# The SSD's new state in another accumulation bank, the first query block's attention on one bank

## The chip, the cores and the metric

The kernel runs on one core of one Trainium2 chip. The metric is device time in microseconds (us) of one execution, as a median of runs; a profile of one execution is there beside it.

## The reference, cut to what matters

One decoder layer over 2048 tokens of width 1024, in float32. Three groups of heads read one shared projection of the normalised input, and their outputs are joined, projected by `w_out` and added to the stream; two more blocks (SwiGLU and a gated embedding) follow.

```python
def _ssd(...):                                 # 6 heads x 64, state 128, chunks of 128
    scores = einsum("bclhn,bcshn->bclsh", cc, bc) * lmat
    y_diag = einsum("bclsh,bcshp->bclhp", scores, xc)
    states = einsum("bclhn,bclh,bclhp->bchpn", bc, decay_s, xc)
    # scan over chunks: carry * dec + st
    y_off = einsum("bclhn,bchpn,bclh->bclhp", cc, prev, exp(acs))
def _forgetting_attention(q, k, v, log_f):     # 6 heads x 64, causal
    logits = q k^T * scale + cum[q] - cum[k];  probs = softmax(masked logits);  out = probs v
...
h = h + concat([y_ssd, y_lru, y_fox]) @ w_out
h = h + (silu(u @ w_gate) * (u @ w_up)) @ w_down
```

## The kernel before, in words

The tokens are worked in four blocks `tb` of 512. Three phases follow each other. `phase1` makes the values, the queries and the RG-LRU for all blocks. `phase1b` runs over the blocks again: it projects `w_xbc`, convolves, runs the SSD in four chunks of 128 tokens (`ssd_chunk`), and makes `w_z` and the keys. `phase3` holds the SwiGLU and the gated embedding, with the attention of query blocks 1 to 3 threaded between its products.

Every large product is made in three passes of 512 columns (high by high, high by low, low by high, lines L201 to L203 in `mm3`, or L214, L215, L219 in `mm3_pair`). These products form the stream of TensorE, written to three accumulation banks with the tag `mm`. The other five banks have one tag each, `xa` to `xe`, and one buffer per tag: whoever writes the bank next waits until the last reader of its content is done.

Attention of query block 0 (`attention(0, ...)`) is a side job. It is started in `phase1b` at `tb == 1` and advanced one step at a time by `Side.tick` while products are recorded. For each of its six heads `scores` handles four query tiles: two products per tile (L642, L643) into the next bank of `tags`, read by VectorE into `lg` with the row's maximum (L647); then maximum, exponential on ScalarE (L654), reciprocal (L656) and scaling (L657). `outputs` takes four key tiles: transposes of `lg` into the next bank (L673), a rounded copy `ph` by ScalarE (L676), the remainder by VectorE (L677), and two products with the values into `xe` (L678, L679). A head ends with L682, L683 and a store to `dy` (L684). The tiles `kx`, `cum`, `lg` and `vc` of a head have one buffer.

`ssd_chunk` uses two banks. In `xa` stand, one after the other, the transposed input (L536, read by L552 and L554), the product with the old state (L563, read by L564) and the new state's product (L568, read by L574); in `xb` stand B by C (L539, L541), the diagonal part (L577) and the transposed result (L584).

At `tb == 3` (the last block) `load_y(0)` is recorded ahead of the SSD chunks. After five of eight tiles it runs `side.finish()`, which records all that is left of the side job, loads the three attention tiles from `dy`, and normalises them (square sums, `rms` in bank `xd`: L139, L141, L143, L145, L151, L153, then L832). The tiles feed `mix`, the product with `w_out`. For its first three output tiles the passes for the first five inputs can run ahead of the attention tiles; all else of the stream from there on stands behind them.

The text of the program doesn't fix the order of the instructions. A scheduler replays the recorded program against its own estimates and lays down one order per engine; each engine then works through its own list strictly in that order.

Of the kernel before, what the change touches and what calls it, by code (L numbers as in the profile page):

```python
# [12 lines left out]
F32R = mybir.dt.float32r  # L13
# [6 lines left out]
P = 128  # L20
# [3 lines left out]
TB = 512  # L24
# [40 lines left out]
class Trunk:  # L65
# [364 lines left out]
    def phase1b(self, ctx):  # L430

        nc, tc, a = self.nc, self.tc, self.a
        pool = lambda name, bufs, **kw: ctx.enter_context(tc.tile_pool(name=name, bufs=bufs, **kw))
        one = pool("m2one", 1)
        two = pool("m2two", 2)
        self.load_mpar(one)
        hcw = self.t(one, [P, 35], "hcw")
        nc.vector.tensor_scalar(hcw, self.pc("scw", 0, 35), 0.5, None, op0=ALU.mult)
        self.neg = self.t(one, [P, P], "neg")
        nc.sync.dma_start(self.neg, a["cst"][:, 2])  # L440
        self.tri = self.t(one, [P, P], "tri")
        nc.sync.dma_start(self.tri, a["cst"][:, 1])
        halo = self.t(one, [P, 7, 3], "halo")
        nc.gpsimd.memset(halo, 0.0)
        state = None
        for tb in range(NTB):
            if tb == 1:
                self.att_setup()
                self.side.start(self.attention(0, one, ("xc", "xd"), "xe"))
            u = []  # L450
            for k in range(KD):
                u.append(self.parts(k, self.load(self.du[tb, k]), nc.gpsimd))
            small = self.decays(tb, two)
            xbc = []
            for b in range(7):
                if b == 0:
                    pair = self.mm3_pair([self.weight(a["w_xbc"][i], KD) for i in range(2)], u)
                ps = pair[b] if b < 2 else self.mm3(self.weight(a["w_xbc"][b], KD), u, 3)
                xbc.append(self.conv(ps, halo[:, b], hcw[:, 4 * b:4 * b + 4], hcw[:, 28 + b:29 + b],
                                     two, (two, f"xbc{b}", 1) if tb % 2 and b else (self.hp, "h", None), True))  # L460
            ys = [self.t(two, [P, TB], f"ys{j}", bufs=1) for j in range(3)]
            if tb == NTB - 1:

                yx = self.load_y(0)
            for c in range(NCH):
                state = self.ssd_chunk(c, xbc, small, state, ys, two)
            if tb == NTB - 1:
                h = [self.mix(0, c, yx) for c in range(KD)]
                self.first = h, self.norm_split(h, "g2", eng=nc.vector, tag="xd")
            for b in range(3):  # L470
                ps = self.mm3(self.weight(a["w_z"][b], KD), u, 3)
                z = self.t(two, [P, TB], "t0")
                nc.scalar.activation(z, ps, ACT.Tanh, scale=0.5)
                nc.vector.scalar_tensor_tensor(z, z, 1.0, ps, op0=ALU.add, op1=ALU.mult)
                nc.vector.scalar_tensor_tensor(ys[b], ys[b], 0.5, z, op0=ALU.mult, op1=ALU.mult)
            for b in range(3):
                self.qk("w_k", b, tb, u, two)
            self.norm_store(ys, 384, 0, tb, "xa")
# [46 lines left out]
    def ssd_chunk(self, c, xbc, small, state, ys, two):  # L525
        nc = self.nc
        cs = slice(c * P, (c + 1) * P)
        xs, bm, cm = xbc[0:3], xbc[3:5], xbc[5:7]
        first = state is None
        dtc, ab, ex = small  # L530
        dt, ab = dtc[:, 0, c], ab[:, c]
        whole, dec, since = ex[:, 0, c], ex[:, 1, c], ex[:, 2, c]

        ptr = self.ps("xa", (P, 3, P))
        for j in range(3):
            nc.tensor.transpose(ptr[:, j], xs[j][:, cs], self.ident)  # L536
        pgb = self.ps("xb", (P, 4, P))
        for g in range(2):
            nc.tensor.matmul(pgb[:, g], lhsT=bm[g][:, cs], rhs=cm[g][:, cs], start=True, stop=True)  # L539
        for g in range(2):  # L540
            nc.tensor.transpose(pgb[:, 2 + g], bm[g][:, cs], self.ident)  # L541
        bt = self.t(two, [P, 2, P], "bt", bufs=1)
        nc.scalar.activation(bt, pgb[:, 2:4], ACT.Copy)

        cb = self.t(two, [P, 2, P], "cb", bufs=1)
        nc.vector.tensor_tensor(cb, pgb[:, 0:2], self.tri.unsqueeze(1).to_broadcast([P, 2, P]), op=ALU.mult)
        seg = self.t(two, [P, 6, P], "seg", bufs=1)
        nc.scalar.activation(seg, ab, ACT.Exp, scale=-1.0)

        px = ptr.rearrange("p j (i e) -> p (j i) e", i=2)  # L550
        xc = self.t(two, [P, 6, 64], "xc", bufs=1)
        nc.vector.tensor_tensor(xc, px, dt.unsqueeze(2).to_broadcast([P, 6, 64]), op=ALU.mult)  # L552
        xd = self.t(two, [P, 6, 64], "xd", bufs=1)
        nc.vector.tensor_tensor(xd, px, dec.unsqueeze(2).to_broadcast([P, 6, 64]), op=ALU.mult)  # L554
        for g in range(2):
            nc.gpsimd.tensor_tensor(seg[:, 3 * g:3 * g + 3], seg[:, 3 * g:3 * g + 3],
                                    cb[:, g].unsqueeze(1).to_broadcast([P, 3, P]), op=ALU.mult)

        yt = self.t(two, [P, 6, 64], "yt", bufs=1)
        if not first:  # L560
            pso = self.ps("xa", (P, 6, 64))
            for g in range(2):
                nc.tensor.matmul(pso[:, 3 * g:3 * g + 3], lhsT=cm[g][:, cs], rhs=state[:, 3 * g:3 * g + 3], start=True, stop=True)  # L563
            nc.vector.tensor_tensor(yt, pso, since.unsqueeze(2).to_broadcast([P, 6, 64]), op=ALU.mult)  # L564

        pst = self.ps("xa", (P, 6, 64))
        for g in range(2):
            nc.tensor.matmul(pst[:, 3 * g:3 * g + 3], lhsT=bt[:, g], rhs=xd[:, 3 * g:3 * g + 3], start=True, stop=True)  # L568
        ns = self.t(two, [P, 6, 64], "state")
        if first:  # L570
            nc.vector.tensor_copy(ns, pst)
        else:
            nc.gpsimd.tensor_tensor(ns, state, whole.unsqueeze(2).to_broadcast([P, 6, 64]), op=ALU.mult)
            nc.vector.tensor_tensor(ns, ns, pst, op=ALU.add)  # L574
        psd = self.ps("xb", (P, 6, 64))
        for h in range(6):
            nc.tensor.matmul(psd[:, h], lhsT=seg[:, h], rhs=xc[:, h], start=True, stop=True)  # L577
        if first:
            nc.vector.tensor_copy(yt, psd)
        else:  # L580
            nc.vector.tensor_tensor(yt, yt, psd, op=ALU.add)
        py = self.ps("xb", (P, 3, P))
        for j in range(3):
            nc.tensor.transpose(py[:, j], yt[:, 2 * j:2 * j + 2].rearrange("p a b -> p (a b)"), self.ident)  # L584
        for j in range(3):
            nc.vector.scalar_tensor_tensor(ys[j][:, cs], xs[j][:, cs], self.pc("dsk", j), py[:, j], op0=ALU.mult, op1=ALU.add)
        return ns
# [20 lines left out]
    def attention(self, qc, pool, tags, tag_o):  # L608
# [52 lines left out]
        def outputs(h):  # L661
# [7 lines left out]
            for kt in range(nkt):  # L669
                d = max(0, kt - qc * NCH)  # L670
                pt = self.ps(next(banks))
                for qi in range(d, NCH):
                    nc.tensor.transpose(pt[:, qi * P:(qi + 1) * P], probs[qi][:, kt * P:(kt + 1) * P], self.ident)  # L673
                sl = slice(d * P, TB)
                ph = self.t(pool, [P, 2, TB], "ph", F32R, bufs=min(3, len(tags)))
                nc.scalar.activation(ph[:, 0, sl], pt[:, sl], ACT.Copy)  # L676
                nc.vector.tensor_tensor(ph[:, 1, sl], pt[:, sl], ph[:, 0, sl].bitcast(F32), op=ALU.subtract)  # L677
                nc.tensor.matmul(po[:, sl], lhsT=vc[:, kt], rhs=ph[:, 0, sl], start=kt == 0, stop=False)  # L678
                nc.tensor.matmul(po[:, sl], lhsT=vc[:, kt], rhs=ph[:, 1, sl], start=False, stop=kt == nkt - 1)  # L679
                yield  # L680
# [7 lines left out]
        for h in range(6):  # L688
            yield from outputs(h)
            if h < 5:  # L690
                yield from scores(h + 1)
# [345 lines left out]
```

## Time and profile before

| what | value |
|---|---|
| median of 3 runs | 2848.45 us (2848.25 to 2850.45) |
| profiled execution, time | 2852.96 us |
| its span, first to last instruction | 2851.1 us |
| TensorE busy | 2745.6 us, 96% of the span |
| mean granted TensorE clock | 0.981 |
| `phase1b` in the trace | from about 300 to about 780 us |
| attention of block 0 | first product at 385.0 us, last at 648.3 us |
| VectorE, ScalarE, GpSimd busy | 53%, 46%, 53% |

The span is 1.9 us shorter than the profiled execution's own time, and that time is 4.5 us above the median. "PEclk" in a row of stretches is the clock that TensorE was granted, as a share of the full one. A row of a timeline gives start, duration, engine, line, operation, tiles, and in brackets the idle time of the engine before it and what ended it.

### The profile page before, as it was taken

To read this page: it belongs to the slowest core of one execution; us is meant where nothing else is said; L and a number is where in the kernel's file an instruction comes from. 1 tells how busy PE (TensorE), PEld (TensorE's weight loads), DVE (VectorE), ACT (ScalarE), POOL (GpSimd) and SP (SyncE) were. 2 spreads that over 40 slices of the span, in tenths; PEclk is the share of its full clock that TensorE was granted. 3 is DMA by queue.
4 is the path that set the end of the run, shared out by engine and by line. 5 is a ranking of instruction groups with operands and counts; after the bars stand their busy time and mean duration, and the time that the engine had idled before them with its cause. 6 is when DMAs were issued, how large, how long until landed. Compare 5 with 4: busy or idle time off the path is not lost.

```text
span 2851.1 us, 36994 instructions
## 1 busy us (share of the span) xinstructions
PE 2745.6 (96%) x12845; PEld 2285.6 (80%) x12845; DVE 1506.5 (53%) x2740; ACT 1299.5 (46%) x1977; POOL 1518.6 (53%) x1409
## 2 busy tenths in 40 slices
PE   7999999998999999999999999999899999999997
PEld 5877787787877888888788888878788888888886
DVE  6776446676544442547655435566564565412236
ACT  5555535544344543434555434446564443322234
POOL 6435677555544555554555645445356554544554
PEclk8999999998999999999999999999999999999999
DMA  5554544352367663434988734279896532322232
GB/s 186 184 182 143 181 165 152 119 157 95 126 199 212 199 191 122 138 126 145 260 238 256 216 112 151 102 218 276 260 268 203 164 133 103 126 97 97 96 98 72
DMA packets 319509, 467.97 MB, mean 164 GB/s; under 512 B 54196, under 2 KB 212948, under 8 KB 317780
## 3 DMA queue, kind: packets, MB, share of 16 engines
q1 hardware_dynamic: 319322, 465.60, 52.5%
q8 instruction: 102, 1.67, 0.2%
q14 instruction: 85, 0.70, 0.1%
HBM read 371.62 MB, written 93.88 MB: 163 GB/s over the span
## 4 chain that ended last, share of the span: by engine, by line
PE 71%; DMA 9%; DVE 6%; POOL 4%; ACT 4%; issue 3%; SPq 2%; DVEq 0%; POOLq 0%; ACTq 0%
PE mm L201 20%; PE mm L202 20%; PE mm L203 20%; POOL w L192 2%; DMA dp<-lg 1%; PE xd L793 1%; PE xd L792 1%; ACT ab L522 1%; PE mm L219 1%; DMA ab<-drow 1%; DMA kx<-dk 1%; PE mm L214 1%; PE mm L215 1%; ACT w L189 1%; POOL u L228 1%
## 5 line engine op out<-in xcount | busy, mean ns | idle before, releaser
L192 POOL TENSOR_TENSOR w<-wst,w 128x512 fp32r<-128x512 f32 x848 | 1148.5, 1377 | 896.1 <-ACT w L189 815.0
L201 PE MATMUL mm<-u,w 128*128 128x512 f32 (+1 forms) x3080 | 1207.2, 392 | 6.9 <-DVE h L489 3.6
L202 PE MATMUL mm<-u,w 128*128 128x512 f32 (+1 forms) x3080 | 1206.1, 392 | 0.6 <-DVE u L879 0.6
L203 PE MATMUL mm<-u,w 128*128 128x512 f32 (+1 forms) x3080 | 1204.9, 392 | 0.8 <-POOL w L192 0.8
L201 PEld LDWEIGHTS mm<-u,w 128*128 128x128 f32 x3080 | 582.5, 189 | 119.2 <-ACT u L227 2.2
L203 PEld LDWEIGHTS mm<-u,w 128*128 128x128 f32 x3080 | 582.2, 189 | 117.0 <-POOL w L192 1.9
L189 ACT ACTIVATE w<-wst 128x1024 fp32r<-128x1024 f32 (+1 forms) x424 | 440.2, 1039 | 512.6 <-PE mm L203 329.7
L202 PEld LDWEIGHTS mm<-u,w 128*128 128x128 f32 x3080 | 582.5, 189 | 109.8 <-DVE u L879 1.0
L788 ACT ACTIVATE ph<-pT 128x512 fp32r<-128x512 f32 (+2 forms) x234 | 119.1, 539 | 146.6 <-PE xd L793 68.7
L789 POOL TENSOR_TENSOR ph<-pT,ph 128x512 fp32r<-128x512 f32 (+2 forms) x108 | 119.7, 1115 | 106.3 <-ACT ph L788 82.8
L789 DVE TENSOR_TENSOR ph<-pT,ph 128x512 fp32r<-128x512 f32 (+2 forms) x126 | 110.2, 888 | 109.5 <-ACT ph L788 99.9
L165 DVE TENSOR_TENSOR ssq<-ssq,sq 128x512 f32<-128x512 f32 x125 | 123.9, 991 | 77.1 <-ACT sq L161 73.9
L879 DVE SCALAR_TENSOR_TENSOR u<-th,u 128x512 fp32r<-128x512 f32 x88 | 111.9, 1271 | 66.8 <-ACT u L878 66.8
L747 ACT ACTIVATE lg<-lg,m 128x1024 f32<-128x1024 f32 (+5 forms) x72 | 102.0, 1416 | 90.1 <-DVE m L745 89.0
L876 DVE TENSOR_TENSOR th<-th,mm 128x512 f32<-128x512 f32 x88 | 60.0, 682 | 155.7 <-PE mm L203 154.9
L751 DVE STREAM_TRANSPOSE lg<-lg 128x1024 f32<-128x1024 f32 (+5 forms) x72 | 113.4, 1576 | 42.9 <-ACT lg L750 42.7
L875 DVE SCALAR_TENSOR_TENSOR th<-th,mm 128x512 f32<-128x512 f32 x88 | 60.1, 682 | 130.7 <-ACT th L874 130.7
L874 ACT ACTIVATE th<-mm 128x512 f32<-128x512 f32 x88 | 52.3, 594 | 162.2 <-PE mm L203 161.0
L892 DVE TENSOR_TENSOR h<-h,mm 128x512 f32<-128x512 f32 x96 | 65.2, 681 | 102.8 <-PE mm L203 102.6
L792 PE MATMUL xd<-ph,vc 128*128 128x256 f32 (+1 forms) x396 | 106.8, 282 | 9.9 <-ACT ph L788 7.0
L793 PE MATMUL xd<-ph,vc 128*128 128x256 f32 (+1 forms) x396 | 103.4, 286 | 3.4 <-DVE ph L789 3.2
L750 ACT ACTIVATE lg<-lg,r 128x1024 f32<-128x1024 f32 (+5 forms) x72 | 101.7, 1412 | 10.7 <-DVE r L749 10.7
(319 smaller groups left out, 3313.7 us busy)
## 6 DMA issues: line engine op xcount, KB each, us to landing
wst<-in_w_gate SPq DMA_DIRECT2D x88, 512.0 KB, 3.7
wst<-in_w_up SPq DMA_DIRECT2D x88, 512.0 KB, 3.6
pT<-dp SPq DMA_DIRECT2D x162, 256.0 KB, 4.5
wst<-in_w_down SPq DMA_DIRECT2D x64, 448.0 KB, 3.5
wst<-in_w_out SPq DMA_DIRECT2D x32, 512.0 KB, 3.5
wst<-in_w_down SPq DMA_DIRECT2D x32, 512.0 KB, 5.4
wst<-in_w_pg SPq DMA_DIRECT2D x32, 512.0 KB, 3.5
vc<-dv SPq DMA_DIRECT2D x60, 256.0 KB, 4.8
```

Source lines behind the costliest of these rows:

```text
L165: (eng or nc.gpsimd).tensor_tensor(acc, acc, s, op=ALU.add)
L189: nc.scalar.activation(w[:, 0], st, ACT.Copy)
L192: nc.gpsimd.tensor_tensor(w[:, 1, k], st[:, k], w[:, 0, k].bitcast(F32), op=ALU.subtract)
L201: nc.tensor.matmul(ps, lhsT=w[:, 0, k], rhs=x[:, 0], start=k == 0, stop=False)
L202: nc.tensor.matmul(ps, lhsT=w[:, 0, k], rhs=x[:, 1], start=False, stop=False)
L203: nc.tensor.matmul(ps, lhsT=w[:, 1, k], rhs=x[:, 0], start=False, stop=k == len(u) - 1)
L751: nc.vector.transpose(lg, lg)
L788: nc.scalar.activation(hi, src, ACT.Copy)
L789: (nc.vector if t0 % 4 == 0 else nc.gpsimd).tensor_tensor(lo, src, hi.bitcast(F32), op=ALU.subtract)
L792: nc.tensor.matmul(po[:, sl], lhsT=vc[:, t0 + i], rhs=ph[:, 0, i, sl], start=t0 + i == 0, stop=False)
L793: nc.tensor.matmul(po[:, sl], lhsT=vc[:, t0 + i], rhs=ph[:, 1, i, sl], start=False, stop=t0 + i == KH - 1)
L879: nc.vector.scalar_tensor_tensor(hh[:, 1], th, 0.5, hh[:, 0].bitcast(F32), op0=ALU.mult, op1=ALU.subtract)
```

## The change

The product for the SSD's new state (L568) goes to bank `xd`, where it went to `xa`. The attention of query block 0, which used `xc` and `xd` in turn, uses `xc` alone. `ph` has two buffers, as it had (the smaller of 3 and the number of banks, which was 2). No arithmetic changes.

```diff
-                self.side.start(self.attention(0, one, ("xc", "xd"), "xe"))
+                self.side.start(self.attention(0, one, ("xc",), "xe"))
...
-        pst = self.ps("xa", (P, 6, 64))
+        pst = self.ps("xd", (P, 6, 64))
...
-                ph = self.t(pool, [P, 2, TB], "ph", F32R, bufs=min(3, len(tags)))
+                ph = self.t(pool, [P, 2, TB], "ph", F32R, bufs=2)
```

The scheduler lays down another order from the first of these instructions on. Three places follow; in the names, the first number is the tile's, and `h` and `xbc` are conv outputs, `lg0` to `lg3` the probabilities of the four query tiles.

TensorE, the outputs of the third head (its sum is `xe_911`), before: the transposes for two key tiles go to `xc` and `xd` in turn, in one piece at the end of a product of `mm_1201`.

```order
L568 MATMUL xa_858_4348<-xd_855_4339,bt_851_4331 128x192 x2
L577 MATMUL xb_860_4354<-xc_854_4337,seg_853_4335 128x64 x6
L673 MATMUL xc_912_4560<-ident_11_92,lg0_879_4452 128x128
L673 MATMUL xc_912_4560<-ident_11_92,lg1_886_4476 128x128
L673 MATMUL xd_914_4576<-ident_11_92,lg1_886_4476 128x128
L673 MATMUL xc_912_4560<-ident_11_92,lg2_893_4498 128x128
L673 MATMUL xd_914_4576<-ident_11_92,lg2_893_4498 128x128
L584 MATMUL xb_861_4362<-ident_11_92,yt_856_4343 128x128 x3
L673 MATMUL xc_912_4560<-ident_11_92,lg3_904_4534 128x128
L673 MATMUL xd_914_4576<-ident_11_92,lg3_904_4534 128x128
L678 MATMUL xe_911_4559<-ph_913_4565,vc_910_4557 128x512
L679 MATMUL xe_911_4559<-ph_913_4565,vc_910_4557 128x512
```

The same head's outputs now; the second key tile's transposes stand behind the first one's L679, and the SSD's L568 has its own bank.

```order
L536 MATMUL xa_1153_5541<-ident_11_92,h_1011_4985 128x128
L678 MATMUL xe_911_4559<-ph_913_4565,vc_910_4557 128x512
L568 MATMUL xd_1149_5520<-xd_1146_5511,bt_1142_5503 128x192 x2
L679 MATMUL xe_911_4559<-ph_913_4565,vc_910_4557 128x512
L673 MATMUL xc_914_4576<-ident_11_92,lg1_886_4476 128x128
L673 MATMUL xc_914_4576<-ident_11_92,lg2_893_4498 128x128
L673 MATMUL xc_914_4576<-ident_11_92,lg3_904_4534 128x128
L536 MATMUL xa_1153_5541<-ident_11_92,h_1015_5002 128x128
```

It moved from behind the 1704th product pass of `phase1b`'s and `phase1`'s stream to behind the 1844th.

TensorE, the end of the stream that can run ahead of the attention tiles (`mm_1401`, third tile of `mix`), before. All of attention lies ahead of these rows; behind them follow the norm of block 2's SSD output (`xa_1227`), one SSD chunk, and the attention tiles' norm (`xd_1325`, `xd_1330`).

```order
L203 MATMUL mm_1401_6699<-u4_1318_6384,w_1400_6695 128x512
L139 MATMUL xa_1227_5917<-ones_14_97,ssq_1224_5909 128x1 x4
...
L563 MATMUL xa_1344_6455<-state_1176_5617,xbc5_1295_6294 128x192
L563 MATMUL xa_1344_6455<-state_1176_5617,xbc6_1302_6342 128x192
L139 MATMUL xd_1325_6401<-ones_14_97,ssq_1322_6393 128x1 x4
L568 MATMUL xa_1345_6459<-xd_1342_6450,bt_1338_6442 128x192 x2
L584 MATMUL xb_1348_6473<-ident_11_92,yt_1343_6454 128x128 x3
```

The same place now: the rest of the fourth head (`xe_966`) and all of the fifth (`xe_1074`) and sixth (`xe_1193`) stand between `mm_1401`'s last early pass and the attention tiles' norm, with no product of the stream among them.

```order
L203 MATMUL mm_1401_6699<-u4_1318_6384,w_1400_6695 128x512
L678 MATMUL xe_966_4779<-ph_1023_5038,vc_965_4777 128x256
...
L642 MATMUL xc_1041_5117<-kx_1034_5102,qx_1036_5104 128x128
...
L679 MATMUL xe_1074_5235<-ph_1089_5313,vc_1073_5233 128x128
L642 MATMUL xc_1105_5376<-kx_1098_5361,qx_1100_5363 128x128
...
L679 MATMUL xe_1193_5685<-ph_1205_5750,vc_1192_5683 128x128
L139 MATMUL xd_1325_6401<-ones_14_97,ssq_1322_6393 128x1 x4
L153 MATMUL xd_1330_6414<-sq_1331_6415,ones_14_97 128x512
L153 MATMUL xd_1330_6414<-sq_1332_6418,ones_14_97 128x512
L201 MATMUL mm_1391_6629<-u5_1333_6422,w_1390_6625 128x512
```

The sixth head ended 68 passes ahead of `mm_1401`'s early end, and now ends behind it.

SyncE's queue, the last attention stores and the load of the last attention tile, now; before, the two stores lay with four loads of weights and one of `ab` between them.

```order
L665 DMA vc_1192_5683<-dv_3_83 128x4x128
L684 DMA dy_4_84<-ot_1090_5324 64x512
L684 DMA dy_4_84<-ot_1206_5761 64x512
L817 DMA ld_1321_6391<-dy_4_84 128x512
L817 DMA ld_1388_6621<-in_xt 128x512
```

The load of the last tile stands directly behind the last store; what moved is where in time the queue comes to them.

## The prediction

> **What bounds the kernel.** I read the page first, then the stretches around the change, then TensorE's timeline in them. The page says who carries the end: TensorE is busy for 96% of the span and holds 71% of the chain that ended last, so whatever adds to its idle or slow time is added to the end, and nothing else is.
>
> ```profile
> PE 2745.6 (96%) x12845; PEld 2285.6 (80%) x12845; DVE 1506.5 (53%) x2740; ACT 1299.5 (46%) x1977; POOL 1518.6 (53%) x1409
> PE 71%; DMA 9%; DVE 6%; POOL 4%; ACT 4%; issue 3%; SPq 2%; DVEq 0%; POOLq 0%; ACTq 0%
> ```
>
> The stretches of the second phase (start:end, length, busy time of the engines, granted clock, DMA share, GB/s) show where TensorE isn't saturated there.
>
> ```profile
> core 0: us, PE busy (x) PEld busy (x) DVE busy (x) ACT busy (x) POOL busy (x), PEclk, DMA share, GB/s
> 430.00:550.00 120.00, 117.12 (x589) 98.33 (x587) 76.17 (x180) 61.07 (x133) 83.16 (x120) 0.99 0.45 142
> 550.00:580.00 30.00, 23.71 (x103) 18.25 (x103) 25.36 (x63) 17.05 (x34) 15.33 (x14) 0.83 0.46 133
> 580.00:650.00 70.00, 68.34 (x363) 58.44 (x362) 46.53 (x122) 33.23 (x74) 37.15 (x61) 0.98 0.51 159
> 650.00:670.60 20.60, 18.00 (x81) 14.94 (x81) 15.46 (x27) 14.52 (x32) 12.63 (x19) 0.92 0.24 71
> 670.60:692.50 21.90, 15.47 (x67) 12.10 (x66) 14.25 (x30) 4.29 (x8) 6.18 (x5) 0.69 0.10 37
> ```
>
> The last row is the hole that matters. At 670.6 us the passes that need no attention tile are used up, and until 692.5 us TensorE has only the norm of the SSD output and one SSD chunk. Its two ends on TensorE, with the chain that closes it:
>
> ```profile
> 670.41 0.39 PE L203 MATMUL mm<-u,w 128*128 128x512 f32 x1
> 675.56 0.79 PE L153 MATMUL xa<-sq,ones 128*128 128x512 f32 x1 [0.85 <-DVE sq L151]
> 679.97 2.79 PE L577 MATMUL xb<-xc,seg 128*128 128x64 f32 x12 [0.74 <-DVE xc L552]
> 683.94 1.71 PE L139 MATMUL xd<-ones,ssq 128*128 128x1 f32 x8
> 692.49 0.97 PE L201 MATMUL mm<-u,w 128*128 128x512 f32 x3 [0.37 <-ACT u L171]
> ```
>
> So the hole lasts 692.49 - 670.64 = 21.9 us (670.64 is where the next instruction took over). Attention had ended well before it, and none of its work is in it.
>
> **The change, part by part.**
>
> The arithmetic, the instructions and their sizes stay. The buffer count of `ph` was 2 and is 2: nothing.
>
> *The SSD's own bank.* L568 no longer waits for L564, and the next chunk's L536 no longer for L574. The order shows the chunks 20 to 80 passes earlier in block 1, and up to 26 in block 2. They are side work beside a saturated stream, so this earns only what TensorE loses around them (below).
>
> *One bank for attention.* Each step must now go product, read, next product, where two banks let the next product run beside the read. In the order the third head's outputs fall back by 140 passes, and the rest of the fourth head with all of the fifth and sixth lands in the hole, with no pass of the stream to hide it. What is late next is the whole stream: `mix` needs the attention tiles. I price the new hole from row durations. By form (busy, mean ns), the steps of a head are:
>
> ```profile
> L647 DVE CUSTOM_DVE_ANT_0 lg<-xc,cd 128x128 f32<-128x128 f32 x12 | 3.4, 284 | 6.7 <-PE xe L679 6.5 <-POOL cd L634 0.2
> L647 DVE CUSTOM_DVE_ANT_0 lg<-xc,cum 128x256 f32<-128x256 f32 x6 | 2.5, 414 | 0.8 <-PE xc L643 0.7
> L647 DVE CUSTOM_DVE_ANT_0 lg<-xd,cum 128x384 f32<-128x384 f32 x6 | 3.3, 548 | 0.2 <-PE xd L643 0.2
> L654 ACT ACTIVATE lg<-lg,m 128x512 f32<-128x512 f32 x6 | 4.3, 722 | 7.0 <-DVE m L652 7.0
> L657 DVE TENSOR_SCALAR lg<-lg,r 128x512 f32<-128x512 f32 x6 | 5.2, 870 | 0.1
> L676 ACT ACTIVATE ph<-xc 128x512 fp32r<-128x512 f32 x6 | 3.6, 595 | 12.3 <-PE xc L673 12.3
> L676 ACT ACTIVATE ph<-xd 128x128 fp32r<-128x128 f32 x6 | 1.6, 274 | 0.7 <-PE xd L673 0.6
> L677 DVE TENSOR_TENSOR ph<-xc,ph 128x512 fp32r<-128x512 f32 x6 | 4.1, 687 | 2.9 <-ACT ph L676 2.9
> L677 DVE TENSOR_TENSOR ph<-xd,ph 128x128 fp32r<-128x128 f32 x6 | 1.7, 279 | 0.0
> L682 ACT ACTIVATE ot<-xe 64x512 f32<-64x512 f32 x6 | 3.6, 595 | 5.9 <-PE xe L679 5.8
> L683 DVE TENSOR_TENSOR ot<-xe,ot 64x512 f32<-64x512 f32 x6 | 4.1, 678 | 2.5 <-ACT ot L682 2.5
> ```
>
> TensorE's steps depend on its clock. In the timeline passes of 512 columns start 0.43 us apart after an idle stretch and 0.23 us apart when it is full; a lone pass of 512 lasts 0.79, so its result is out 0.36 us after its columns are through (0.17 by 0.40 at full clock).
>
> ```profile
> 554.67 0.79 PE L678 MATMUL xe<-ph,vc 128*128 128x512 f32 x1 [0.47 <-ACT ph L676]
> 561.45 0.63 PE L201 MATMUL mm<-u,w 128*128 128x512 f32 x1
> 561.88 0.63 PE L202 MATMUL mm<-u,w 128*128 128x512 f32 x1
> 565.41 0.40 PE L203 MATMUL mm<-u,w 128*128 128x512 f32 x1
> 565.64 0.39 PE L201 MATMUL mm<-u,w 128*128 128x512 f32 x1
> ```
>
> Scores of one head at half clock: products 2 x (0.11 + 0.21 + 0.32 + 0.43) + 4 x 0.36 = 3.6; reads, with the diagonal tile's 0.284 each time, 0.28 + 0.57 + 0.70 + 0.83, and 0.08 four times for the maximum = 2.7; the last tile's exponential 0.72 (with 0.4 for maximum, sum and reciprocal) and scaling 0.87 = 2.0. Outputs: transposes 1.1 + 4 x 0.36 = 2.5; the copies 0.60 to 0.27, summed along the sizes 1.7; the remainders 0.69 to 0.28, summed 1.9; the second products behind them 1.1 + 0.36 = 1.4. Some 20 hand-overs at 0.05 (the rows above start that much after their releaser ends) add 1.0. One head: 3.6 + 2.7 + 2.0 + 2.5 + 1.7 + 1.9 + 1.4 + 1.0 = 16.8 us. At full clock 4.5 less for the columns and results: 12.3.
>
> The hole then reads:
> - Until the fifth head's first product: the fourth head's end runs beside the norm, whose second L153 ends 676.35 - 670.64 = 5.7 after the stream; with the last remainder, 6.2.
> - The fifth head, 16.8, and the SSD chunk that its steps are interleaved with: L577 2.8 and three or four more small products of about 1 each, partly beside VectorE: 6.
> - The sixth head: 16.8.
> - The end: L682 0.6, L683 0.7, store 2.4, load 3.3, square and sum 1.4, and from L139 to the first pass 692.49 - 683.94 = 8.6: 17.0. The DMA rows (issue of the store and of the load that waits for it; the load's median to landing; and the issue of `cum`, ns, with its landing):
>
> ```profile
> 655.46 0.47 SPq L684 DMA_DIRECT2D dy<-ot  x1
> 657.81 0.33 SPq L817 DMA_DIRECT2D ld<-dy  x1
> ld<-dy SPq DMA_DIRECT2D x32, 256.0 KB, 3.3
> L628 SPq DMA_DIRECT2D cum<-dcum x6: 332/520/529, 385.4 to 605.4; - x6
> DMA to landing us min/median/max: 3.9/4.1/5.7
> ```
>
> That is 6.2 + 16.8 + 6 + 16.8 + 17.0 = 62.8 us at half clock, and 6.2 + 12.3 + 4 + 12.3 + 17.0 = 51.8 at full clock. The hole of before ran at 0.69 with a fuller TensorE, so I take 61, near the half-clock end. Upwards: the sixth head's keys load only once the fifth's scores are done, seven issues of about 0.5 us and some 4 us of landing against the 7.6 us of outputs that cover them; if these loads or slow forms of L657 come on top, 68. The term is 61 - 21.9 = **+39** (30 to 46).
>
> The Trainium skill ("TensorE: Matmul & The Clock Gate", Part 1) says that TensorE falls to half its clock after one idle window of about 3.4 us and needs as long a busy one to return. By that rule nearly all of this hole runs at half clock and the term is 41, by a gate that never closes it is 30. The 0.69 of the old hole agrees with a mixture that leans to the closed gate.
>
> *Work that leaves the covered part.* What the hole now does, the stream ahead of it no longer does. A head has 26 attention products; in the stream four of the smaller scores take 0.51 us together (592.91 to 593.42 below), so about 0.13 each, and the larger ones up to 0.23.
>
> ```profile
> 592.91 0.27 PE L642 MATMUL xc<-kx,qx 128*128 128x128 f32 x1
> 593.42 0.33 PE L577 MATMUL xb<-xc,seg 128*128 128x64 f32 x2
> ```
>
> 26 x 0.146 = 3.8 us per head, for 2.35 heads: **-8.9** (6.8 by columns alone to 11). One L568 and one L563 pair leave the hole for the later stream: **+0.8**.
>
> *Stalls ahead of the hole.* From 430 to 670.6 us TensorE idles 2.9 + 6.3 + 1.7 + 2.6 = 13.5 us, and the missing share of the clock, times the busy time, is 1.2 + 4.0 + 1.4 + 1.4 = 8. Half of that, 10.3, is in the one bunch of 550 to 580, which is exactly where the order shows the two-bank outputs piled up (TensorE waited there for `lg`, `ph` and `yt`). That bunch is dissolved. New bunches with one bank cost something back, because L679 now stands ahead of the next transposes in the list. **-8** (0 to -16).
>
> *GpSimd's list.* The next head's mask (L634) waits for `cum`, and the split of a weight of `mix` (L192) stands behind it. Fewer heads are done by then, so the waits fall among the passes that end the stream: **+2** (0 to 4).
>
> Sum: 39 - 8.9 + 0.8 - 8 + 2 = **+25 us**. The profiled execution would go from 2852.96 to 2878; against the median of the runs, 2848.45, I expect 2873.5. The ends together: 30 - 11 + 0.8 - 16 = +4, and 46 - 6.8 + 0.8 + 0 + 4 = +44; both ends need every term at its bound, so the range is 2856 to 2892.
>
> **The rivals.**
>
> A. *Keys and GpSimd stack up*: a wait takes the removed one's place at each head, for `cum` and `kx`. For it: in this trace each head loads its keys into the only buffer. Against it: seven issues fit in the outputs of one head. It gives 2892 to 2905.
>
> B. *The gate stays open and the stalls vanish*: the hole at full clock (+30) and all of the saving (-16) with -8.9 and +0.8 give +6, about 2854: the edge of no change.
>
> C. *Not slower: the unblocked SSD chunks empty the stalls ahead of the hole.* Place: 430 to 670 us. Price: at most the 21.5 us that the rows show, plus the 8.9 moved. It decides when the stalls saved exceed 39 - 8.9 + 0.8 = 31, and the rows hold only 21.5; only with the hole at its lower bound (30 - 8.9 + 0.8 = 22) do they meet. So about 2843 to 2850, and unlikely.
>
> D. *The second bank was never used*, since products are released by the ticks and not by banks. Then nothing ends later, and the time is within 0.2%. Against it stands the order, in which attention already ends late. The Trainium skill (the same page, "HAM oscillation") tells of a kernel in which double-buffering the accumulation banks gave no further gain (126.6 us to 125.5); the same here would mean about 2848.
>
> **How the numbers follow.** A measurement of this kernel can tell about 0.2% (5.7 us) from no change. Forecast, +8 to +44: 0.82. A: 0.07. B: 0.05, of which 0.02 lies within 0.2%. C: 0.04, of which 0.03 faster by more than 0.2%. D: 0.02, no change. Slower 0.92, same 0.05, faster 0.03. The range of 2856 to 2892 leaves out A, C, D and most of B.
>
> **What would show it.** Right: in the new profile a stretch of some 60 us, from about 650 to 715, in which TensorE is busy a third to a half with a clock of 0.5 to 0.7, chained L673, L676, L677, L679 and ended by L171; the stretch 550 to 580 fuller than before; all later stretches as before. Wrong: a hole under 50 us, attention's last L679 ahead of the last early pass of `mix`, or idle time in the third phase that isn't there now.

## The result, and the profile after

The changed kernel takes 2874.54 us (median of four runs, 2874.2 to 2875.35) against 2848.74 us: a ratio of 1.0089, 95% interval 1.0076 to 1.0102, so 25.8 us slower. The forecast was 2873.5. The profiled execution took 2874.38 us with a span of 2872.5.

The engines' totals hardly move; TensorE has the same 12845 products in 9 us more busy time, and its share of the chain falls from 71% to 68%.

```profile
PE 2754.8 (96%) x12845; PEld 2291.1 (80%) x12845; DVE 1498.5 (52%) x2740; ACT 1300.4 (45%) x1977; POOL 1519.2 (53%) x1409
PE 68%; DMA 10%; DVE 7%; ACT 5%; POOL 4%; issue 3%; SPq 2%; DVEq 0%; ACTq 0%; POOLq 0%
```

The stretches of the second phase, after (columns as in the prediction), with the new gap in the last row:

```profile
320.00:430.00 110.00, 104.07 (x487) 86.20 (x486) 48.72 (x97) 51.44 (x106) 78.95 (x116) 0.95 0.48 153
...
430.00:550.00 120.00, 115.86 (x565) 96.01 (x564) 78.55 (x165) 61.39 (x130) 87.89 (x121) 0.97 0.43 142
550.00:580.00 30.00, 30.00 (x151) 25.30 (x150) 17.04 (x39) 14.72 (x27) 15.44 (x16) 1.00 0.38 127
580.00:650.00 70.00, 67.36 (x348) 57.29 (x346) 49.17 (x115) 36.59 (x82) 45.79 (x75) 0.95 0.49 153
650.00:659.00 9.00, 9.00 (x50) 7.79 (x49) 6.10 (x14) 5.50 (x11) 2.21 (x3) 1.00 0.01 2
659.00:717.30 58.30, 32.85 (x102) 21.49 (x100) 26.14 (x88) 13.86 (x34) 6.16 (x10) 0.56 0.19 57
```

550 to 580 is full now. The gap is 58 us long, with TensorE busy 56% of it at a clock of 0.56. TensorE's timeline through it: the last early pass, the first product of the fifth and of the sixth head, the sixth head's last product, the attention tiles' norm, and the pass that ends the gap.

```profile
658.81 0.39 PE L203 MATMUL mm<-u,w 128*128 128x512 f32 x1
...
661.00 0.30 PE L642 MATMUL xc<-kx,qx 128*128 128x128 f32 x1
...
683.06 0.58 PE L679 MATMUL xe<-ph,vc 128*128 128x256 f32 x1
683.44 0.41 PE L673 MATMUL xc<-ident,lg 128*128 128x128 f32 x1
684.22 0.47 PE L678 MATMUL xe<-ph,vc 128*128 128x128 f32 x1 [0.37 <-ACT ph L676]
684.55 0.47 PE L679 MATMUL xe<-ph,vc 128*128 128x128 f32 x1
684.82 0.41 PE L642 MATMUL xc<-kx,qx 128*128 128x128 f32 x1
...
701.60 0.47 PE L679 MATMUL xe<-ph,vc 128*128 128x128 f32 x1
710.11 1.87 PE L139 MATMUL xd<-ones,ssq 128*128 128x1 f32 x8 [8.03 <-DVE ssq L165]
714.43 1.30 PE L153 MATMUL xd<-sq,ones 128*128 128x512 f32 x2 [2.45 <-DVE sq L151]
717.26 1.65 PE L201 MATMUL mm<-u,w 128*128 128x512 f32 x3 [1.53 <-ACT u L171]
```

With 0.23 for the last pass, the gap runs from 659.04 to 717.26: 58.2 us against 21.9. It ends 24.8 us later than before (717.26 - 692.49); the spans differ by 21.4.

### The profile page after: what moved, and what is told of

It reads as the page before. It is cut to its first block, busy times and chain, and to the rows that moved or that the text cites. A ratio compares the mean times of both kernels' runs of the same rounds, so it can differ in the third digit from the quotient of the medians.

```text
span 2872.5 us, 36967 instructions
## 1 busy us (share of the span) xinstructions
PE 2754.8 (96%) x12845; PEld 2291.1 (80%) x12845; DVE 1498.5 (52%) x2740; ACT 1300.4 (45%) x1977; POOL 1519.2 (53%) x1409
## 4 chain that ended last, share of the span: by engine, by line
PE 68%; DMA 10%; DVE 7%; ACT 5%; POOL 4%; issue 3%; SPq 2%; DVEq 0%; ACTq 0%; POOLq 0%
PE mm L201 19%; PE mm L203 19%; PE mm L202 19%; DMA dp<-lg 2%; POOL w L192 2%; PE xd L793 1%; PE xd L792 1%; DMA pT<-dp 1%; DMA kx<-dk 1%; ACT ab L522 1%; DMA wst<-in_w_up 1%; PE mm L219 1%; DMA ab<-drow 1%; PE mm L214 1%; PE mm L215 1%
## 5 line engine op out<-in xcount | busy, mean ns | idle before, releaser
L201 PE MATMUL mm<-u,w 128*128 128x512 f32 (+1 forms) x3080 | 1208.9, 393 | 7.1 <-DVE h L489 4.6
L201 PEld LDWEIGHTS mm<-u,w 128*128 128x128 f32 x3080 | 583.2, 189 | 119.1 <-ACT end L486 2.8
```

Source lines behind the costliest of these rows:

```text
L201: nc.tensor.matmul(ps, lhsT=w[:, 0, k], rhs=x[:, 0], start=k == 0, stop=False)
```

## The experiments

One theory was that the whole loss is attention's single bank, which leaves two heads in the gap. The rival put part of it on the state's own bank. The table has, for each kernel, the start of the last pass that needs no attention tile, the start of the first that needs one, the gap (start of the second less that of the first, less 0.23), and the times against the kernel before on the same chip. That kernel's median was 2848.74 us beside the changed kernel, and 2851.17, 2850.00 and 2852.05 us on the three chips of the other kernels.

| kernel | last early pass | first pass with the tile | gap | median, us | ratio, 95% interval |
|---|---|---|---|---|---|
| before | 670.41 | 692.49 | 21.9 | | |
| changed | 658.81 | 717.26 | 58.2 | 2874.54 | 1.0089 (1.0076 to 1.0102) |
| changed, once more | 658.07 | 715.95 | 57.7 | 2878.93 | 1.0093 (1.0079 to 1.0107) |
| one bank, state in xa | 653.79 | 715.20 | 61.2 | 2865.95 | 1.0052 (1.0035 to 1.0069) |
| the same, once more | 654.24 | 715.63 | 61.2 | 2865.34 | 1.0044 (1.0031 to 1.0057) |
| two banks, state in xd | 693.48 | 717.20 | 23.5, and 29.0 ahead of it | 2878.33 | 1.0094 (1.0074 to 1.0114) |
| two banks, state in xb | 688.99 | 711.99 | 22.8, and 17.4 ahead of it | 2869.72 | 1.0064 (1.0049 to 1.0079) |
| changed, four heads | 654.99 | 679.84 | 24.6 | 2841.94 | 0.9968 (0.9957 to 0.998) |
| before, four heads | 664.78 | 686.87 | 21.9 | 2849.55 | 0.9995 (0.9984 to 1.0006) |
| first head on one bank | 670.20 | 686.81 | 16.4 | 2845.65 | 0.9982 (0.9971 to 0.9994) |
| scores xc, outputs xd | 664.62 | 687.62 | 22.8 | 2842.03 | 0.9966 (0.9953 to 0.9979) |
| changed, two key products ahead | 672.61 | 722.37 | 49.5 | 2878.60 | 1.0093 (1.0068 to 1.0118) |
| first head on one bank, two keys ahead | 686.61 | 689.88 | 3.0 | 2840.72 | 0.9967 (0.9953 to 0.998) |
| first head on one bank, one key ahead | 675.32 | 686.90 | 11.4 | 2837.81 | 0.9946 (0.9931 to 0.996) |

### The two heads in the gap

The two kernels with four heads leave the fifth and sixth head out and store ones in their place:

```diff
-        for h in range(6):
+        for h in range(4):
             yield from outputs(h)
-            if h < 5:
+            if h < 3:
                 yield from scores(h + 1)
+        for h in (4, 5):
+            ot = self.t(pool, [64, TB], "ot")
+            nc.vector.memset(ot, 1.0)
+            nc.sync.dma_start(self.dy[5 + h // 2, 64 * (h % 2):64 * (h % 2) + 64, tsl], ot)
+            yield
```

On the changed kernel:

> The changed kernel with only heads 0 to 3 of the first query block's attention computed (ones are stored for the fifth and sixth), so that the two heads that stand uncovered are gone. Theory (the uncovered heads are the loss): the gap from the last early pass to the first pass with the attention's tile falls from 58 us to 18 to 26 us, the time to 2830 to 2846 us, and this kernel is within 5 us of the kernel before with the same two heads left out. Rival (the loss lies in what the single bank does to the covered heads, or in the SSD's chunks, and the gap only moves): it stays 15 to 26 us behind the kernel before with the two heads left out.

On the kernel before:

> The kernel before with only heads 0 to 3 of the first query block's attention computed (ones are stored for the fifth and sixth). It is what the changed kernel with the same heads left out is compared with. The attention then ends well ahead of the last early pass of the mix; the two heads' products, some 7 to 9 us of TensorE, are gone from the covered part. Theory: gap 18 to 24 us, time 2836 to 2846 us. Rival (the covered heads cost the stream more than their products, by the stalls ahead of the gap): 2815 to 2835 us.

Without the two heads the changed kernel is 7.6 us *faster* than the kernel before without them (2841.94 against 2849.55). Its gap falls from 58.2 to 24.6. So the loss needs the two heads, and with them gone the change shows a gain that the gap otherwise covers. It lies in the 550 to 580 bunch. First the kernel before with four heads, then the changed kernel with four:

```profile
550.00:580.00 30.00, 23.81 (x101) 18.10 (x100) 25.59 (x71) 17.70 (x37) 16.44 (x16) 0.77 0.38 105
```

```profile
550.00:580.00 30.00, 30.00 (x155) 25.57 (x155) 18.22 (x43) 12.92 (x23) 14.89 (x15) 1.00 0.47 153
```

At full clock that is 30.0 against 23.81 x 0.77 = 18.3 us of product time: 11.7 us, of which the 2.7 us longer gap takes some back. The bunch is still there in the kernel before although the last two heads are gone. The measured 7.6 is beyond the 5 us that I allowed, on the side of the changed kernel. The kernel before gains almost nothing by losing two heads (1.6 us, within its interval), and so lies above the 2836 to 2846 us expected. By the profiles its gap begins 5.6 us earlier (664.78 against 670.41) and ends 5.6 us earlier (686.87 against 692.49), and its span is 3.4 us shorter (2847.7 against 2851.1); where the rest of the two heads' 7 to 9 us went isn't shown.

### The halves apart

Attention on one bank, the state left in xa (run twice, the second time beside the changed kernel on one chip):

```diff
-        pst = self.ps("xd", (P, 6, 64))        # the changed kernel
+        pst = self.ps("xa", (P, 6, 64))
```

> The attention goes through one bank as in the changed kernel, but the SSD's new state is written to its old bank xa, so xd is used by nobody. Theory (the loss comes from the attention's single bank: the fifth and sixth head run after the last early pass of the mix, where TensorE has nothing to stand beside them): in the order both heads still start after that pass, so the gap from the last early pass to the first pass with the attention's tile stays at 50 to 62 us against 22 before, and the time is 2865 to 2882 us. Rival (the SSD's bank of its own costs the time, by what it moves on VectorE and TensorE): the time falls back to 2846 to 2853 us and the gap to about 22 us.

> The changed kernel once more, on the same chip as the kernel with attention on one bank and the new state in its old bank xa, to compare the two halves. Theory (all of the loss is attention's single bank): both have the same gap (58 and 61 us) and both lie 18 to 28 us above the kernel before, less than 5 us apart. Rival (the state's own bank, given the single bank, costs time of its own): the changed kernel is 7 to 12 us above the other.

> Attention on one bank, the new state in its old bank xa, once more, beside the changed kernel on the same chip. Theory: 18 to 28 us above the kernel before, within 5 us of the changed kernel. Rival: 12 to 17 us above the kernel before and 7 to 12 us below the changed kernel.

The gap is there in full (61.2 us) with the single bank alone, so the first half of the theory holds. But that kernel is only 13.3 us above the kernel before (2865.34 - 2852.05), and the changed kernel on the same chip 26.9. The state's own bank costs the other 13.6 us: the rival's answer, and more than its 7 to 12. It doesn't cost them in the gap, since both gaps end within 0.3 us of each other. The spans of the two differ by 13.9 us (2875.6 and 2861.7), all of it behind the gap. What is done there differs. The new state's product L568, by stretch (ahead of the gap, in it, behind it: busy time and count, clock, DMA), with the state in xa:

```profile
320.00:655.00 335.00, 10.10 (x48) 0.98 0.46 144
655.00:716.00 61.00, 4.35 (x16) 0.75 0.19 54
716.00:1000.00 284.00, 0.00 (x0) 0.99 0.63 187
```

and in the changed kernel, once more:

```profile
320.00:655.00 335.00, 10.06 (x48) 0.98 0.47 146
655.00:716.00 61.00, 0.00 (x0) 0.61 0.19 54
716.00:1000.00 284.00, 3.92 (x16) 0.98 0.61 180
```

With the state in xa the last block's four SSD chunks run beside the two heads. With the state in xd none of these 16 products runs there. The whole chunks follow: of the 80 SSD products that the orders list for that block, all stand in the gap in the first kernel and none behind it; in the second 21 stand in it, 55 behind it and 4 ahead of it. Behind the gap TensorE is saturated (busy all of the first 50 us there in the changed kernel), so each of the 55 takes time from the stream; their busy times there, read in the same way line by line (L536, L539, L541, L563, L568, L577, L584), add up to 15.1 us. In the kernel before 51 of the 80 stand behind its gap too. So the state's own bank hardly adds work behind the gap; it withholds what the single bank alone would have gained by drawing that work into the gap.

The order shows why. The attention tiles' norm also writes xd, and the program records it ahead of these chunks, so a bank's next user waits for it. In the changed kernel:

```
L139 MATMUL xd_1325_6401<-ones_14_97,ssq_1322_6393 128x1 x4
L153 MATMUL xd_1330_6414<-sq_1331_6415,ones_14_97 128x512
L153 MATMUL xd_1330_6414<-sq_1332_6418,ones_14_97 128x512
...
L568 MATMUL xd_1345_6459<-xd_1342_6450,bt_1338_6442 128x192 x2
```

In the kernel with the state in xa, the four L568 of this block stand ahead of that L139. In the trace of the changed kernel's second run the first of them comes right behind the gap:

```profile
713.12 1.30 PE L153 MATMUL xd<-sq,ones 128*128 128x512 f32 x2 [2.45 <-DVE sq L151]
715.95 1.65 PE L201 MATMUL mm<-u,w 128*128 128x512 f32 x3 [1.53 <-ACT u L171]
717.40 1.48 PE L568 MATMUL xd<-xd,bt 128*128 128x192 f32 x4
```

So the bank "of its own" is shared with the one norm that has to wait for all of attention. No run gives that norm another bank, which would have tested this directly; the cause rests on the order and on these rows.

The other half, two banks for attention and the state in xd, shared with the scores:

```diff
-        pst = self.ps("xa", (P, 6, 64))        # the kernel before
+        pst = self.ps("xd", (P, 6, 64))
```

> The other half alone: the SSD's new state is written to bank xd, and the attention keeps its two banks xc and xd, so that scores and state share xd. Theory (it is the attention's single bank that costs): in the order the first five heads start ahead of the last early pass of the mix and only the sixth head's end stands behind it; the gap there is 20 to 30 us and the time 2843 to 2858 us. Rival (the new state in xd costs the time): 2865 to 2880 us, with the gap no longer than before.

My reading missed: 2878.33 us, with the gap itself at 23.5, but with 29.0 us more without a product of the stream, ending 6 us ahead of it.

```profile
658.38 0.39 PE L203 MATMUL mm<-u,w 128*128 128x512 f32 x1
...
677.55 0.80 PE L642 MATMUL xd<-kx,qx 128*128 128x512 f32 x1 [1.66 <-DVE state L574]
...
685.56 0.48 PE L673 MATMUL xc<-ident,lg 128*128 128x128 f32 x1 [4.07 <-DVE lg L657]
...
687.59 0.80 PE L201 MATMUL mm<-u,w 128*128 128x512 f32 x1 [1.34 <-DVE t L474]
```

SSD chunk and head now take turns in xd (the scores L642 wait for the state's reader L574), and the stream stands until VectorE's L474 has read the bank of a `w_z` product. I had looked at the rows behind the last early pass, and not at the 33 rows in one place 15 passes ahead of it. That the shared bank is what brought them together is argued from the order; the rows show one wait for the state's reader, of 1.66 us, and a longer one for `lg`. The expectation's rival (that xd is the costly place) has the time right, but the gap isn't "no longer than before" as it said: there are two.

The halves don't add up, then. The state's bank alone costs 27.2 us (2878.33 - 2851.17), and attention's single bank on top of it nothing (26.9 for both). The 13.3 and 13.6 us are the prices of the two steps in the one order only, attention's bank first.

And with the state in xb:

```diff
-        pst = self.ps("xa", (P, 6, 64))
+        pst = self.ps("xb", (P, 6, 64))
```

> The kernel before with the new state written to bank xb in place of xa; attention keeps xc and xd for itself. The state's product then no longer waits for the old state's readers in xa, but shares xb with the diagonal part. In the order the heads start earlier than before, the same 27 rows stand behind the last early pass of the mix, and one pile of 34 rows of attention and SSD stands at one pass of the stream (17 before). Theory (gap and piles are what counts, the bank of the state by itself is worth nothing): gap 20 to 24 us as before, a longer stall where the pile is, 2846 to 2858 us. Rival (the state's wait in xa cost the SSD's chunks and with them the stream): 2836 to 2846 us.

Both readings missed: 2869.72 us, 17.7 above the kernel before. The gap is the old one (22.8), but 17.4 us are lost ahead of it, here in TensorE's rows:

```profile
666.69 0.39 PE L203 MATMUL mm<-u,w 128*128 128x512 f32 x1
...
674.07 1.65 PE L568 MATMUL xb<-xd,bt 128*128 128x192 f32 x4 [6.33 <-DVE cb L546]
676.53 2.79 PE L577 MATMUL xb<-xc,seg 128*128 128x64 f32 x12 [0.81 <-DVE state L574]
...
684.30 0.79 PE L201 MATMUL mm<-u,w 128*128 128x512 f32 x1 [3.43 <-DVE t L474]
```

L539, L568, L577 and L584 now pass through xb one behind the other, and the last chunk of block 2 stands uncovered; the stream waits for L474 again, which stands behind that chunk in VectorE's list. But the long wait, 6.33 us, is hardly the bank's. On VectorE:

```profile
668.31 0.18 DVE L514 COPY ex<-ab 128x24 f32<-128x24 f32 x1 [3.96 <-DMA ab<-drow]
...
673.59 0.42 DVE L546 TENSOR_TENSOR cb<-xb,tri 128x256 f32<-128x256 f32 x1 [3.07 <-ACT bt L543]
```

The load of `ab` came late, ScalarE's exponentials of it (L522) waited 8.15 us for L514, and L543, which makes the `bt` that L568 needs in any bank, stands behind them and ended at 673.49. L568 started at 674.07, so the bank's part is at most 0.6 us. What set the chunk there without a pass beside it stays open. The pile of 34 rows that I had pointed at is elsewhere. Both banks that I gave the state in place of xa cost time.

### Who uses which of two banks

The first head on one bank, the others on two:

```diff
-                    ps = self.ps(next(banks))
+                    ps = self.ps(next(banks) if h else tags[0])
...
-                pt = self.ps(next(banks))
+                pt = self.ps(next(banks) if h else tags[0])
```

> The kernel before, with the first head alone on one bank (xc); heads two to six alternate between xc and xd as before, and the new state stays in xa. In the order the first head's outputs fall back, the piles of attention and SSD rows at two passes of the stream (17 and 16 rows) are spread to at most 13, and behind the last early pass of the mix stand 21 rows in place of 27. Theory (what counts is where TensorE's side work finds no product of the stream beside it, not the number of banks): the stall from 550 to 580 us mostly goes, the gap at the last early pass is 14 to 21 us against 22, and the time is 3 to 12 us below the kernel before, 2837 to 2847 us. Rival (a second bank is worth something for every head, so that each head on one bank costs a sixth of the 20 to 26 us): 2850 to 2856 us.

Two banks with fixed roles:

```diff
-                    ps = self.ps(next(banks))
+                    ps = self.ps(tags[0])
...
-                pt = self.ps(next(banks))
+                pt = self.ps(tags[1])
```

> The kernel before, with scores always through xc and the transposed probabilities always through xd: two banks again, but none of the two chains alternates within itself. The new state stays in xa. In the order the heads begin no later than before, the largest pile has 12 rows, and behind the last early pass stand 29 rows with the sixth head's end among them. Theory (the loss comes from scores and outputs of neighbouring heads that stand in one line on the single bank, and so from heads left for the gap): gap 22 to 30 us, time 2840 to 2854 us. Rival (what pays is the alternation within one chain, so that product and read overlap): as slow as one bank, 2862 to 2876 us.

Both theories hold. The first kernel gives 0.9982 (4.4 us in the medians), barely outside no change, with the gap 5.5 us shorter; the second gives 0.9966, 8.0 us in the medians, with the gap 0.9 us longer. Alternation within a chain is not what a second bank is worth. What it is worth is that the next head's scores needn't stand in one line with this head's outputs. With fixed roles the 550 to 580 row is full as well:

```profile
550.00:580.00 30.00, 30.00 (x144) 24.58 (x143) 25.72 (x58) 15.54 (x32) 17.98 (x25) 0.97 0.32 100
```

### Passes put into the gap

Some of the last block's key products recorded ahead of the mix (two here, one in the last run):

```diff
             if tb == NTB - 1:
+                for b in range(2):
+                    self.qk("w_k", b, tb, u, two)
                 h = [self.mix(0, c, yx) for c in range(KD)]
...
-            for b in range(3):
+            for b in range(2 if tb == NTB - 1 else 0, 3):
                 self.qk("w_k", b, tb, u, two)
```

On the changed kernel:

> The changed kernel, with two of the last block's three key products (48 passes of the stream, 11 us) recorded ahead of the mix in place of behind it. The fifth and sixth head still stand behind the last pass that needs no attention tile. Theory (the loss is time without a product of the stream beside the heads): part of the heads' chain now runs beside these 48 passes, the gap falls from 58 us to 44 to 54 us, and the time is 4 to 14 us below the changed kernel, 2860 to 2870 us. Rival (the heads' chain only starts later with the passes ahead of it, so the gap keeps its length): gap 56 to 60 us, 2871 to 2878 us.

On the kernel before with its first head on one bank, with two key products and with one:

> The kernel before, with the first head alone on one bank and two of the last block's three key products recorded ahead of the mix. All of attention and of the SSD then lies ahead of the last pass that needs no attention tile. Theory (the gap is what costs): gap 2 to 10 us, and the time 10 to 22 us below the kernel before, 2827 to 2840 us. Rival (the passes taken from behind the mix uncover the norm ahead of the third phase): the gap closes, but 5 to 15 us of idle time appear at the start of the third phase, near 760 us, and the time is 2838 to 2850 us.

> The kernel before, with the first head alone on one bank and one of the last block's three key products recorded ahead of the mix, in place of two as in the run with two. 11 rows stand behind the last early pass, and some 70 passes of the stream stay between the norm ahead of the third phase and that phase, against 76 before. Theory: the gap is 5 to 12 us, and the 5 us of idle time at the start of the third phase that two key products brought are gone or down to 1; 2832 to 2842 us, the best of the kernels so far. Rival (what the gap gives is given back in the third phase in any case): 2842 to 2850 us.

On the changed kernel the gap falls by 8.7 us as the theory said, and the time doesn't move (1.0093): neither expectation holds whole. 48 passes of 0.23 are 11 us fewer behind the gap, its end is 5.1 us later (722.37 - 717.26), which leaves 5.9 to gain; and at the start of the third phase, where the changed kernel's TensorE is full, 42.4 - 38.9 x 0.96 = 5.1 us are lost. In the changed kernel with two keys ahead:

```profile
780.00:822.40 42.40, 38.90 (x168) 31.72 (x168) 23.80 (x38) 16.24 (x24) 17.70 (x14) 0.96 0.46 136
```

The kernel with the first head on one bank and two keys ahead shows what is given back, first on TensorE, then on VectorE (its lines behind the inserted two are numbered two higher than before's):

```profile
780.12 0.50 PE L201 MATMUL mm<-u,w 128*128 128x512 f32 x1 [2.72 <-DVE th L877]
```

```profile
776.74 1.88 DVE L255 TENSOR_TENSOR sq<-ys,xa 128x512 f32<-128x512 f32 x3 [4.82 <-PE xa L153]
...
779.38 1.28 DVE L877 SCALAR_TENSOR_TENSOR th<-th,mm 128x512 f32<-128x512 f32 x2 [0.55 <-ACT th L876]
```

L877 (the third phase's first gate) frees the bank that L201 waits for, and stands on VectorE behind L255, the last step of `norm_store`, which waits 4.82 us for its own norm. With one key product left between, that norm isn't done in time. So the rival had the size (5.2 us by its row below) and the phase, but the wrong norm: SSD's output, not the stream's. With one key product ahead in place of two it is gone; the same stretch, first with two, then with one:

```profile
750.00:790.00 40.00, 35.20 (x159) 28.64 (x158) 23.91 (x35) 15.33 (x23) 17.60 (x13) 0.99 0.51 146
```

```profile
750.00:790.00 40.00, 40.00 (x184) 33.25 (x183) 24.38 (x40) 14.27 (x20) 17.10 (x14) 1.00 0.58 177
```

The theory holds, and that kernel is faster than both kernels of this study's question: 2837.81 us, 0.9946 of the kernel before (0.9931 to 0.996), 14.2 us. By the profiles 5.6 are the gap's earlier end (692.49 - 686.90) and 5.5 the 24 passes that no longer follow it; the spans differ by 16.1 (2851.1 - 2835.0), so 5.0 more lie behind the gap, where no row names them.

## Why the prediction came out right

The sum was +25; the run medians say +25.8, the two profiled executions +21.4 (before's lay 4.2 us above its median of 2848.74, after's at its own). That the medians come within 0.8 us of the sum is partly luck: in the profiles the three terms below miss by -2.7, +3.3 and -4.2 us, in all -3.6, and the profile of before, lying above its median, hides that. By its terms, in the profiles:

- **The hole, +39 (30 to 46): measured +36.3** (58.2 - 21.9). Its parts: until the fifth head's first product 2.0 (6.2 predicted; the norm of the SSD output began ahead of the last passes, so it no longer held the start), the fifth head with the SSD chunk 23.8 (22.8), the sixth head 17.2 (16.8), the end 15.2 (17.0). The heads were priced well from rows of other stages; the start was mis-sized. The bound of 30 was too low by the prediction's own figures: from half to full clock a head's columns save 2.0 us (4.3 to 2.3) and its nine results 1.7 (0.36 to 0.17 each), 3.7 in all and not 4.5, which makes the hole 53.4 and the bound 31.5.
- **Work that leaves the covered part (-8.9), GpSimd's list (+2), stalls ahead (-8).** Together -14.9; the gap begins 11.6 us earlier (670.64 - 659.04). The stalls, as length less busy time times clock, fall from 430 us on from 21.4 to 13.6: -7.8, and the bunch of 550 to 580 is the part that goes, as said. What I left out is 320 to 430, where the loss rises from 6.6 (before, the row below) to 11.1: +4.5. I can't lay that on the order: in the changed kernel's second profile it is 7.2 there (110 - 102.77 x 1.00). The remaining -8.3 answers to -8.9 and +2, which I didn't measure apart.

```profile
320.00:430.00 110.00, 105.51 (x503) 87.40 (x502) 50.96 (x97) 53.28 (x108) 80.07 (x121) 0.98 0.48 157
```

- **L568 and L563 leave the hole, +0.8.** The count is right against the kernel before: 55 SSD products behind the gap against 51. Behind it the changed kernel's profile is 3.4 us shorter (2155.2 against 2158.6), a difference that no term names and that isn't the change's: its second profile has 2159.7 us there, and in the eight kernels with the same passes behind the gap and SSD products there, that stretch lay between 2154 and 2161 us.

So 36.3 - 11.6 - 3.4 = 21.3, the span difference.

One step was right in its number and wrong in its reason. "The SSD's own bank" was held to earn or cost nothing beyond the stalls, and the whole +39 was laid on attention's bank. The runs say that the single bank alone costs 13.3 us, since the gap that it opens can be filled with the SSD chunks, and that the state's bank is what keeps them out, 13.6 us. The other way round the state's bank costs it all. My sum came out because it was read from the order with both halves in place; read from the diff half by half it would have been wrong. Of the signs, one is off: TensorE was busy 56% of the gap, above the third to a half that I named.

Rival A didn't come: the sixth head took 17.2 us, and TensorE waited for no load in it (in the fifth once, 0.64 us). Rival C needed 31 us of stalls saved; they fell by 7.8, or with 320 to 430 by 7.8 - 4.5 = 3.3. Rival D is refuted by the single bank's own 13.3 us. Rival B needed an open gate: the granted clock over the gap was 0.56, and 0.50 in the stretches shown at the end. The Trainium skill ("TensorE: Matmul & The Clock Gate", Part 1) let the term be 41 by a gate that falls to half. Measured were 36.3, and the clock agrees: it was 0.50 from 674 us to the end of the gap, with the sixth head at 17.2 us against the half-clock price of 16.8. For the fall the Trainium skill names there an idle window of about 3.4 us; in this trace no wait of TensorE in the gap up to then was longer than 1.86 us (last section). The Trainium skill (the same page, "HAM oscillation") tells of a kernel in which a second set of accumulation banks gave no further gain (126.6 us to 125.5). This kernel differs: with the state in xa, one bank in place of two costs 0.44% (0.31 to 0.57).

## What to carry to other kernels

A bank is only a chain's own if nobody else's program order runs through it: list every user of a bank in the order of the program, and look for one that waits for something late (here a norm behind all of attention). When side work is moved out from under a saturated stream, find the point where the stream stands, and ask both what lands there and what can still share it. Filling such a gap with later passes pays only as far as those passes weren't covering something where they stood: one key product paid, two gave some 5 us back.

## What the hardware showed that I hadn't expected

TensorE's clock fell to half without a long pause. From 680 to 700 us in the changed kernel it was busy 64% of the time, its longest idle wait from 659 to 702 us was 1.86 us, and the granted clock was 0.50. First the row with that wait, then the stretches:

```profile
671.74 0.55 PE L584 MATMUL xb<-ident,yt 128*128 128x128 f32 x3 [1.86 <-DVE yt L581]
...
680.00:690.00 10.00, 6.45 (x16) 4.13 (x17) 4.58 (x21) 3.07 (x9) 1.82 (x4) 0.50 0.15 39
690.00:700.00 10.00, 6.27 (x16) 3.03 (x14) 3.69 (x12) 2.65 (x7) 0.00 (x0) 0.50 0.00 1
```

With the SSD chunks among the same heads (state in xa, second run) the same stretches were busier and ran near full clock:

```profile
680.00:690.00 10.00, 8.19 (x56) 6.90 (x54) 8.49 (x37) 3.90 (x10) 4.02 (x6) 1.00 0.16 41
690.00:700.00 10.00, 7.06 (x37) 4.74 (x36) 5.25 (x15) 2.92 (x7) 2.20 (x2) 0.95 0.00 1
```

At 63% of busy time the clock was 0.50, at 71% 0.95. No limit between them can be read from this: busy time itself stretches at a lower clock (in the prediction's rows a pass of 512 lasts 0.79 us after an idle stretch and 0.40 when TensorE is full), and from 668 to 674 us in the changed kernel TensorE was busy 60% of the time at a clock of 0.78. The 59 more products of the order fit into a gap only 3 us longer. TensorE idled 25.4 us of the changed kernel's gap (58.30 - 32.85), so part of them only fill idle time; what the faster clock adds wasn't measured apart.
